# A decoder layer on one core: smaller blocks in the delta rule's substitution, and the memory keys worked out earlier

## The chip, the core and the metric

The kernel runs on one core of a Trainium2 chip. The time is the device time of one execution in microseconds. Three runs of the kernel before took 1222.79, 1224.20 and 1224.33 us; the median is 1224.2 us. The profile is of one execution, whose span is 1222.4 us.

## The reference

One layer of a hybrid decoder works on 512 tokens of 1024 channels, in float32. Each part is h = h + weight * rms_norm(part(rms_norm(h))). The parts are, in order: a SwiGLU feed-forward network with an inner width of 2816; a mixer; a cross-attention into 256 memory tokens (4 heads of 256); and a second feed-forward network.

The mixer has two groups of heads. Eight heads of 64 do causal softmax attention with a forget gate ("fox"). Four heads of 128 follow the gated delta rule, here over chunks of tokens:

```
L = strict_lower((k * beta) @ k.T) * decay       # per head and chunk
A = I + L
u = solve(A, v * beta);  w = solve(A, k * beta * exp(g))
for each chunk:
    v_new = u - w @ state
    o     = (q * exp(g)) @ state + attn_intra @ v_new
    state = state * exp(g_last) + k_tail.T @ v_new
```

The memory keys are the first half of rms_norm(mem) @ mem_w_kv. They depend on the memory tokens and weights alone, not on h.

## The kernel before, in words

The layer lies in SBUF as four blocks of 128 tokens: `h[0]` to `h[3]`, each 128 x 1024. Every product is float32 made of three passes over float32r parts: each weight block (128 x 1024, 512 KB) is loaded into `raw`, and split into a high part `wh` (ScalarE) and a low part `wl` (VectorE, or GpSimd for every second block where `nblock[1]` is 2; lines 431 to 436). `raw` has three buffers, `wh` and `wl` four each, and they go round in the order in which the program names the blocks, whatever the order of the work.

The order of the work is not the program's. The class `Issue` keeps every instruction with what it reads and writes, and at the end `settle` places them on the engines by assumed durations (lines 160 to 179 and `AFTER`) in ten rounds of list scheduling, and fixes the order in which each engine and the SP queue issue. On the chip an engine issues in that order: an instruction that is ready waits behind one that is not. Work on one PSUM bank stays in program order.

The mixer stage is, in program order:

- Gates: the first weight block gives the gate logits; a chain of small VectorE instructions on `gw` ends in `yd`, which TensorE transposes.
- For each of four delta heads: the keys' product, a convolution (`cy`, `cth`, `co`), and `L`, four chunks of 128 x 128 side by side.
- The inverse of A. `L` of each head is written to DRAM (`dl`), and its 32 x 32 diagonal blocks are read back into `Lb`, a block to a partition, 64 partitions for four heads, four chunks and four blocks (lines 983 to 987). Forward substitution on all 64 blocks at once takes 31 steps of two VectorE instructions, on `Wb` and `Tb` (lines 992 to 998). `inverse(hh)` writes a head's 16 inverted blocks to DRAM (`dt`, four DMAs), reads them back as `T` in place, transposes to `X`, and doubles the blocks twice by products, 32 to 64 and 64 to 128 rows (lines 1038 to 1092).
- `qv(hh)`: queries and values of a delta head, and its attention inside a chunk. `scan(hh)`: the recurrence over four chunks, a serial chain between TensorE, VectorE and ScalarE. `fox_values`: values of the fox heads.
- These steps stand in program order by `PLAN` (line 30): q0 q1 q2 i0 s0 i1 s1 q3 F0 i2 s2 i3 s3, where q is `qv`, i `inverse`, s `scan`, F `fox_values`.
- Then the fox heads in four pairs, the output gate `gz`, the normed and transposed memory tokens `mT` (lines 1292 to 1317), the output projection `wout`, and h's update.

The cross-attention then works out the memory keys `Km` (8 weight blocks `wkvk`, lines 1337 to 1355), the memory values `Vm` (8 blocks `wkvv`), and the queries, which need the norm of the new h. Keys and values need no h.

Of the kernel before, what the change touches and what calls it, by code (L numbers as in the profile page):

```python
# [16 lines left out]
P = 128  # L17
S = 512
# [20 lines left out]
class Issue:  # L39
    """The order in which the engines issue.  # L40

    Every instruction is kept with what it reads and writes. At the end they are placed on the
    engines by a rough cost, backwards and forwards by turns, of those ready the most urgent
    first, and each engine gets its instructions in that order (as dependencies that need no
    semaphore).
    """

    # from the end of an instruction to the start of one that waits for it: on the same engine,
    # on the tensor engine, on another
# [45 lines left out]
    def cells(self, x):  # L95
        """name, pieces touched, rows, free size"""
# [22 lines left out]
    def add(self, ins, unit, op, fp32):  # L119
# [4 lines left out]
        for group, cells_of, size_of in ((ins.ins, reads, sizes[0]), (ins.outs, writes, sizes[1])):  # L124
            for x in group:
# [5 lines left out]
                if name.startswith("psum"):  # L131
                    # one after another on a bank
# [127 lines left out]
class _Issuer:  # L260
    """an engine whose instructions are kept"""
# [19 lines left out]
def tile_decoder_layer(  # L281
# [23 lines left out]
    cid32: bass.AP,  # L305
# [14 lines left out]
    # slots of [128, 512], handed out by hand  # L320
# [20 lines left out]
    def move(src, dst, n=None):  # L341
        """free slots from one ring to another"""
# [14 lines left out]
    def bank(*ids):  # L357
        """the next PSUM bank of a ring of banks"""
# [20 lines left out]
    # that of some instructions stays as written  # L379
# [33 lines left out]
    def rstd_of(s0, s1):  # L413
        """(s0 + s1 + eps) ^ -1/2"""
# [16 lines left out]
    def wblock(ap):  # L431
        """now and then Pool takes the low part"""
# [10 lines left out]
    # the first loads, in the order in which they are needed  # L443
# [28 lines left out]
    def prenorm(src, g, dst):  # L472
        """rms_norm of a block of 128 rows, transposed and split into dst(half, part)."""
# [78 lines left out]
    def residual_epilogue(gidx, weight, nxt, final=False):  # L552
        """evac callback: h += weight * rms_norm(product) * gain; then nxt(t)."""
# [356 lines left out]
    for hh in range(GH):  # L910
        Q.dma_start(rows_of(dt_[hh]), zb)
# [660 lines left out]
```

## Time and profile before

| what | from the page or the times |
|---|---|
| median of three runs | 1224.2 us |
| span of the profiled execution | 1222.4 us |
| lies around it (1222.79 to 1224.33 less the span) | 0.4 to 1.9 us |
| TensorE matmul busy | 1192.9 us, 98% |
| VectorE busy | 642.7 us, 53% |
| ScalarE busy | 493.0 us, 40% |
| GpSimd busy | 128.6 us, 11% |
| moved by DMA | 120.32 MB, mean 98 GB/s |

Busy time of TensorE is the union of its matmuls, which overlap; a stretch at 20.00 of 20.00 us has no idle time, but is not free of slow matmuls. The stages by time: first feed-forward network to about 377 us, mixer to about 640 us with the delta rule at about 400 to 555 us, output projection to 689 us, cross-attention to about 860 us, second feed-forward network to the end.

### The profile page before, as it was taken

How to read it: one execution, taken by the hardware profiler on the slowest of the kernel's cores; microseconds unless marked ns; L12 is line 12 of the kernel's file. 1: busy time of each engine (PE TensorE's matmuls, PEld its weight loads, DVE VectorE, ACT ScalarE, POOL GpSimd, SP SyncE). 2: the span in 40 equal slices, each digit the busy share in tenths (PEclk: the TensorE clock that was granted, in tenths of full speed). 3: DMA queues.
4: the chain of work that ended last, by engine and by line, in shares of the span. 5: the costliest groups of instructions: out<-in, count | busy, mean ns of one | idle time of the engine just before them, and what ended most of it. 6: DMA issues, size and time to landing. Idle time of an engine off the chain costs nothing.

```text
span 1222.4 us, 15630 instructions
## 1 busy us (share of the span) xinstructions
PE 1192.9 (98%) x6078; PEld 1002.6 (82%) x6078; DVE 642.7 (53%) x1152; ACT 493.0 (40%) x1024; POOL 128.6 (11%) x121
## 2 busy tenths in 40 slices
PE   7999999999999899899999999999999999999997
PEld 7888888888888687788787888888988888888886
DVE  5655455442327979469975744546634334342323
ACT  5323223222226564368974644435422323222221
POOL 1000000000001432222020442012000000000000
PEclk9999999999999999999999999999999999999999
DMA  5332322333333231211214253222432332333321
GB/s 192 122 100 90 103 88 102 103 103 104 109 101 104 87 113 57 91 54 54 73 60 164 91 181 118 79 67 65 125 103 88 102 97 93 104 107 100 102 71 69
DMA packets 41753, 120.32 MB, mean 98 GB/s; under 512 B 9424, under 2 KB 9680, under 8 KB 41680
## 3 DMA queue, kind: packets, MB, share of 16 engines
q1 hardware_dynamic: 41168, 119.20, 30.9%
q8 instruction: 47, 0.77, 0.3%
q0 software_dynamic: 512, 0.13, 0.1%
q14 instruction: 26, 0.21, 0.1%
HBM read 114.73 MB, written 4.46 MB: 98 GB/s over the span
## 4 chain that ended last, share of the span: by engine, by line
PE 87%; DVE 7%; DMA 2%; issue 2%; ACT 2%; SPq 0%; POOL 0%; DVEq 0%; POOLq 0%; ACTq 0%
PE psum L270 87%; DVE Wb L270 1%; DVE Tb L270 1%; DMA mr<-in_mem_dram 1%; DVE wl L270 1%; DVE gw L270 1%; DMA raw<-in_wkvk_dram 1%; DVE co L270 1%; DVE xn L270 1%; DVE cy L270 0%; SPq L270 0%; DMA h<-in_x_dram 0%; DVE smalls L270 0%; DVE pt L270 0%; DVE h L270 0%
## 5 line engine op out<-in xcount | busy, mean ns | idle before, releaser
L270 PE MATMUL psum<-xt,wh 128*128 128x512 f32 (+1 forms) x2064 | 599.4, 374 | 0.3 <-ACT wh L270 0.2
L270 PEld LDWEIGHTS psum<-xt,wh 128*128 128x128 f32 x2064 | 373.6, 190 | 63.5 <-ACT wh L270 0.5
L270 ACT ACTIVATE wh<-raw 128x1024 fp32r<-128x1024 f32 (+1 forms) x202 | 213.0, 1056 | 526.0 <-PE psum L270 293.3
L270 PE MATMUL psum<-xt,wl 128*128 128x512 f32 (+1 forms) x1016 | 376.6, 375 | 0.8 <-DVE wl L270 0.7
L270 DVE TENSOR_TENSOR wl<-raw,wh 128x1024 fp32r<-128x1024 f32 (+1 forms) x176 | 216.3, 1230 | 275.8 <-ACT wh L270 275.2
L270 PEld LDWEIGHTS psum<-xt,wl 128*128 128x128 f32 x1016 | 190.9, 190 | 32.7 <-DVE wl L270 1.2
L270 PE MATMUL psum<-wh,hh 128*128 128x512 f32 x352 | 137.1, 390 | 0.0
L270 PE MATMUL psum<-wl,hh 128*128 128x512 f32 x352 | 137.1, 390 | 0.0
L270 PE MATMUL psum<-wh,hl 128*128 128x512 f32 x352 | 137.0, 389 | 0.0
L270 POOL TENSOR_TENSOR smalls<-smalls,mhalf 128x1 f32<-128x1 f32 (+1 forms) x38 | 26.5, 700 | 789.8 <-ACT smalls L270 784.0
L270 PEld LDWEIGHTS psum<-wh,hh 128*128 128x128 f32 x352 | 66.1, 188 | 13.8
L270 PEld LDWEIGHTS psum<-wh,hl 128*128 128x128 f32 x352 | 66.1, 188 | 13.6
L270 PEld LDWEIGHTS psum<-wl,hh 128*128 128x128 f32 x352 | 66.1, 188 | 13.6
L270 POOL TENSOR_TENSOR wl<-raw,wh 128x1024 fp32r<-128x1024 f32 x26 | 63.7, 2450 | 120.8 <-ACT wh L270 110.2
L270 PE MATMUL psum<-wh,xt 128*128 128x512 f32 x128 | 43.5, 409 | 0.4 <-DVE q L270 0.4
L270 DVE SCALAR_TENSOR_TENSOR hv<-s,psum 128x512 f32<-128x512 f32 x22 | 15.1, 688 | 53.7 <-PE psum L270 53.5
L270 DVE TENSOR_TENSOR tu<-psum,rb 128x512 f32<-128x512 f32 x22 | 15.2, 692 | 53.4 <-PE psum L270 53.3
L270 DVE TENSOR_TENSOR fg<-psum,gbc 128x512 f32<-128x512 f32 x32 | 22.0, 688 | 37.1 <-ACT u L270 37.1
L270 DVE TENSOR_TENSOR tg<-psum,rb 128x512 f32<-128x512 f32 x22 | 15.2, 692 | 44.5 <-PE psum L270 44.5
L270 ACT ACTIVATE u<-psum 128x512 f32<-128x512 f32 x32 | 19.0, 593 | 41.4 <-PE psum L270 41.4
L270 ACT ACTIVATE hh<-hv 128x512 fp32r<-128x512 f32 x44 | 27.4, 623 | 16.2 <-DVE hv L270 16.2
L270 DVE TENSOR_TENSOR hl<-hv,hh 128x512 fp32r<-128x512 f32 x44 | 30.1, 685 | 1.5 <-ACT hh L270 1.5
(232 smaller groups left out, 1431.3 us busy)
## 6 DMA issues: line engine op xcount, KB each, us to landing
raw<-in_f2gu_dram SPq DMA_DIRECT2D x44, 512.0 KB
raw<-in_f1gu_dram SPq DMA_DIRECT2D x43, 512.0 KB
raw<-in_f1d_dram SPq DMA_DIRECT2D x22, 512.0 KB
raw<-in_f2d_dram SPq DMA_DIRECT2D x22, 512.0 KB
raw<-in_wmt_dram SPq DMA_DIRECT2D x21, 512.0 KB
gbc<-in_gains_dram SPq DMA_DIRECT2D x16, 256.0 KB
raw<-in_wmn_dram SPq DMA_DIRECT2D x8, 512.0 KB
raw<-in_wout_dram SPq DMA_DIRECT2D x8, 512.0 KB
```

Source lines behind the costliest of these rows:

```text
L270: r = call(*args, **kw)
```

## The change

The substitution works on 16 x 16 diagonal blocks: 128 blocks, one to each partition, 15 steps instead of 31. The DRAM copies hold the chunks one after another, so that one DMA reads or writes all blocks of a head. `inverse` gets one more doubling ahead of the two, 16 to 32 rows, on 32 x 32 quarters with a mask.

The memory tokens are normed and transposed right after the `L`s, in the buffers of `h`; the memory keys become steps K0 to K3 of `PLAN`, ahead of i2. R0 gives free slots back. For that time h is kept in DRAM: each block is written after the first feed-forward network, and read back ahead of `wout`. The fox values lie in the buffers of h too. NSLOT grows by 3.

The durations that the planner assumes change: 13.3 ns instead of 2.6 ns over the columns for one-pass matmuls, half for four-pass matmuls of up to 32 rows, and 2.04 ns per element for the scan instruction. Comments are taken out.

```diff
-NSLOT = 51
+NSLOT = 54
-PLAN = 'q0 q1 q2 i0 s0 i1 s1 q3 F0 i2 s2 i3 s3'.split()
+PLAN = 'q0 q1 q2 i0 s0 i1 s1 q3 R0 F0 K0 K1 K2 K3 i2 s2 i3 s3'.split()
+KHOME = {}
...
-            cost = max(size * passes * 0.41667, cols * 0.8333) + 2.6
+            cost = max(size * passes * 0.41667, cols * 0.8333) + (13.3 if passes == 1 else 2.6)
+            if passes == 4 and rows <= 32:
+                cost /= 2
...
-            cost = 68 + size * (6.3 if op == "reciprocal" else 0.521 if single else 1.042) + 61 * scalars
+            each = {"reciprocal": 6.3, "tensor_tensor_scan": 2.04}.get(op, 0.521 if single else 1.042)
+            cost = 68 + size * each + 61 * scalars
...
+        def nxt(t):
+            norm(t)
+            kept.append(issue.tile(dram, [P, D], F32, tag="hd", bufs=4, name=nm("hd"), grain=(0, 1024)))
+            Q.dma_start(kept[t], h[t])
...
-        Q.dma_start(rows_of(dl[hh]), L)
-        for c in range(NT):
-            p0 = 16 * hh + 4 * c
-            Q.dma_start(Lb[p0 : p0 + 4], blocks_of(dl[hh], c))
+        Q.dma_start(rows_of(dl[hh]), by_chunk(L))
+        Q.dma_start(Lb[32 * hh : 32 * hh + 32], blocks_of(dl[hh]))
...
+    gkv = issue.tile(pool, [P, D], F32, tag="h0", name=nm("gkv"))
+    xns = issue.tile(pool, [P, D], F32, tag="h3", name=nm("xns"))
+    Q.dma_start(gkv, gains[G_MEMKV : G_MEMKV + 1, :].to_broadcast([P, D]))
+    for t in range(2):
+        mr = issue.tile(pool, [P, D], F32, tag=f"h{1 + t}", name=nm("mr"))
+        Q.dma_start(mr, mem[t * P : (t + 1) * P, :])
...
-    for j in range(31):
-        n = [64, 31 - j, j + 1]
-        w_ = Wb[0:64, 0 : n[1] * n[2]].rearrange("p (r s) -> p r s", s=n[2])
+    for j in range(15):
+        n = [P, 15 - j, j + 1]
+        w_ = Wb[:, 0 : n[1] * n[2]].rearrange("p (r s) -> p r s", s=n[2])
...
-        for c in range(NT):
-            p0 = 16 * hh + 4 * c
-            Q.dma_start(blocks_of(dt_[hh], c), Tb[p0 : p0 + 4])
+        Q.dma_start(blocks_of(dt_[hh]), Tb[32 * hh : 32 * hh + 32])
...
+        quarters = [slice(32 * i, 32 * i + 32) for i in range(4)]
+        qp = pg()
+        for c in range(NT):
+            for b in quarters:
+                mm(qp[b, 32 * c : 32 * c + 32], ck(L, c)[b, b], ck(X, c)[b, b], start=True, stop=True)
+        V.tensor_tensor(c3(Qs[:, 0:P]), c3(qp[:, 0:P]), low16[:, None, :].to_broadcast([P, NT, 32]), ALU.mult)
+        xp = pg()
+        for c in range(NT):
+            for b in quarters:
+                mm(xp[b, 32 * c : 32 * c + 32], ck(T, c)[b, b], Qs[b, 32 * c : 32 * c + 32], start=True, stop=True)
+            for b in quarters[0:3]:
+                mm(xp[b, P + 32 * c : P + 32 * c + 32], Qs[b, 32 * c : 32 * c + 32], ck(T, c)[b, b], start=True, stop=True)
+        for i, b in enumerate(quarters):
+            V.tensor_tensor(c3(X)[b, :, b], c3(X)[b, :, b], c3(xp[:, 0:P])[b], ALU.subtract)
+            if i < 3:
+                V.tensor_tensor(c3(T)[b, :, b], c3(T)[b, :, b], c3(xp[:, P : 2 * P])[b], ALU.subtract)
...
+    def memory_keys(dp):
+        ps = acc()
+        for e in range(2):
+            wh, wl = wblock(wkvk[2 * dp + e])
...
+            Km[0][dp], Km[1][dp] = u(F32R, "km"), u(F32R, "km")
+        split(Km[0][dp], Km[1][dp], ps)
...
+    for t in range(NT):
+        h[t] = issue.tile(pool, [P, D], F32, tag=f"h{t}", name=nm("h"))
+        Q.dma_start(h[t], kept[t])
```

## Rows read from the trace of the kernel before

**Rows 1.** The page: busy time, share and instructions of each engine; GB/s in 40 slices.

```profile
PE 1192.9 (98%) x6078; PEld 1002.6 (82%) x6078; DVE 642.7 (53%) x1152; ACT 493.0 (40%) x1024; POOL 128.6 (11%) x121
...
GB/s 192 122 100 90 103 88 102 103 103 104 109 101 104 87 113 57 91 54 54 73 60 164 91 181 118 79 67 65 125 103 88 102 97 93 104 107 100 102 71 69
```

**Rows 2.** Windows: stretch, length, busy per engine (instructions), granted clock, DMA share, GB/s.

```profile
400.00:420.00 20.00, 15.95 (x83) 13.22 (x82) 19.18 (x46) 11.16 (x32) 5.54 (x5) 0.91 0.29 92
460.00:480.00 20.00, 17.37 (x81) 13.82 (x80) 19.01 (x36) 10.47 (x28) 4.59 (x3) 0.91 0.18 53
500.00:520.00 20.00, 17.64 (x177) 14.12 (x178) 8.32 (x23) 9.09 (x33) 2.34 (x1) 0.91 0.35 113
640.00:660.00 20.00, 19.16 (x96) 15.15 (x95) 13.38 (x22) 9.76 (x21) 2.12 (x4) 1.00 0.67 220
```

**Rows 3.** Timeline of TensorE at its stalls: start, us, instructions, idle time before, what ended it.

```profile
410.80 1.08 PE L270 MATMUL psum<-ident,yd 128*128 128x128 f32 x4 [4.05 <-DVE smalls L270]
463.13 0.49 PE L270 MATMUL psum<-cm 128*128 128x512 f32 x1 [2.63 <-ACT vb L270]
502.32 0.52 PE L270 MATMUL psum<-X,L 32*32 32x32 f32 x8 [3.28 <-DVE X L270]
...
708.97 0.66 PE L270 MATMUL psum<-ident,xn 128*128 128x128 f32 x4 [1.86 <-DVE xn L270]
```

**Rows 4.** Windows of VectorE at the substitution: all of it, then `Tb`'s instructions alone.

```profile
448.00:495.00 47.00, 45.16 (x88) 0.96 0.19 61
...
448.00:495.00 47.00, 29.96 (x62) 0.96 0.19 61
```

**Rows 5.** Timeline of VectorE: steps of the substitution, and what stands between them.

```profile
449.72 0.21 DVE L270 TENSOR_TENSOR Tb<-Tb,Wb 64x60 f32<-64x60 f32 x1
457.39 2.46 DVE L270 TENSOR_TENSOR Wb<-Lb,Tb 64x207 f32<-64x207 f32 x1
459.88 0.37 DVE L270 TENSOR_TENSOR Tb<-Tb,Wb 64x207 f32<-64x207 f32 x1
```

**Rows 6.** Timeline of GpSimd beside it.

```profile
457.11 2.50 POOL L270 TENSOR_TENSOR wl<-raw,wh 128x1024 fp32r<-128x1024 f32 x1
```

**Rows 7.** Timeline of SP after the substitution, and the chain's piece behind it.

```profile
494.96 3.80 SPq L270 DMA_DIRECT2D dt<-Tb  x9
...
498.87 2.65 DMA T<-dt
```

**Rows 8.** TensorE by form, 380 to 620 us; then its timeline around small products.

```profile
L270 PE MATMUL psum<-X,L 32*32 32x32 f32 x64 | 3.4, 196 | 3.3 <-DVE X L270 3.3
...
506.30 0.47 PE L270 MATMUL psum<-X,L 32*32 32x32 f32 x13
506.70 0.51 PE L270 MATMUL psum<-wl,xt 128*128 128x512 f32 x1
507.04 0.63 PE L270 MATMUL psum<-wh,xt 128*128 128x512 f32 x2
```

**Rows 9.** Tiles `mT`, `mr`, `T`: operation, count, ns min/median/max, first and last start.

```profile
L270 PE MATMUL psum<-mT,wh x128: 277/283/365, 689.0 to 716.3; 128*128 128x256 f32 x128
L270 PE MATMUL psum<-wh,mT x64: 389/389/396, 716.5 to 738.1; 128*128 128x512 f32 x64
L270 DVE TENSOR_TENSOR mT<-psum,mT x8: 418/422/425, 649.5 to 654.4; 128x256 fp32r<-128x256 f32 x8
L270 DVE SCALAR_TENSOR_TENSOR xn<-mr,smalls,gbc x4: 743/748/752, 643.4 to 648.8; 128x512 f32<-128x512 f32 x4
L270 DVE TENSOR_SCALAR T<-psum x4: 283/283/284, 506.8 to 538.3; 32x128 f32<-32x128 f32 x4
```

**Rows 10.** Timeline of VectorE where the mixer begins: h's update, weight split, idle time.

```profile
381.12 0.74 DVE L270 SCALAR_TENSOR_TENSOR h<-fg,smalls,h 128x512 f32<-128x512 f32 x1
385.50 1.22 DVE L270 TENSOR_TENSOR wl<-raw,wh 128x1024 fp32r<-128x1024 f32 x1
393.88 0.75 DVE L270 SCALAR_TENSOR_TENSOR cy<-psum,cw,cy 128x511 f32<-128x511 f32 x1 [5.64 <-ACT cth L270]
```

More of the change, by code (lines that the diff above doesn't have):

```diff
@@ L304, in tile_decoder_layer @@
     crow: bass.AP,
-    cid32: bass.AP,
+    cid16: bass.AP,
     out: bass.AP,
@@ L715, in next_norm, with norm_and_store @@
         return nxt
-    ffn(f1gu, f1d, xT, G_F1POST, next_norm(G_MIXPRE), lead=lead_in)
+    kept = []
+    def norm_and_store(gidx):
+        norm = next_norm(gidx)
+        def nxt(t):
+            norm(t)
+            kept.append(issue.tile(dram, [P, D], F32, tag="hd", bufs=4, name=nm("hd"), grain=(0, 1024)))
+            Q.dma_start(kept[t], h[t])
+        return nxt
+    ffn(f1gu, f1d, xT, G_F1POST, norm_and_store(G_MIXPRE), lead=lead_in)
     xT = state["xT"]
@@ L983, in tile_decoder_layer @@
         fr(Dn)
-        Q.dma_start(rows_of(dl[hh]), L)
-        for c in range(NT):
-            p0 = 16 * hh + 4 * c
-            Q.dma_start(Lb[p0 : p0 + 4], blocks_of(dl[hh], c))
+        Q.dma_start(rows_of(dl[hh]), by_chunk(L))
+        Q.dma_start(Lb[32 * hh : 32 * hh + 32], blocks_of(dl[hh]))
         front.append((kT, L, cV, cR, kt))
-    for j in range(31):
-        n = [64, 31 - j, j + 1]
-        w_ = Wb[0:64, 0 : n[1] * n[2]].rearrange("p (r s) -> p r s", s=n[2])
+    mTt = [[[u(F32R, "mT") for _ in range(2)] for _ in range(2)] for _ in range(2)]
+    gkv = issue.tile(pool, [P, D], F32, tag="h0", name=nm("gkv"))
[4 more added lines that the diff above has]
+        Q.dma_start(mr, mem[t * P : (t + 1) * P, :])
+        sq = [small(1) for _ in range(2)]
+        hs = [slice(j * 512, (j + 1) * 512) for j in range(2)]
+        xn = [xns[:, hs[j]] for j in range(2)]
+        for j in range(2):
+            square(mr[:, hs[j]], 1.0 / 32.0, sq[j], xn[j])
+        r = rstd_of(*sq)
+        for j in range(2):
+            V.scalar_tensor_tensor(xn[j], mr[:, hs[j]], r, gkv[:, hs[j]], ALU.mult, ALU.mult)
+            tp = acc()
+            for c in range(4):
+                TE.transpose(ck(tp, c), ck(xn[j], c), ident)
+            t3 = tp.rearrange("p (c q) -> p c q", c=4)
+            for e in range(2):
+                hi, lo = (
+                    mTt[j][q_][e].rearrange("p (c q) -> p c q", c=2)[:, :, t * P : (t + 1) * P] for q_ in range(2)
+                )
+                split(hi, lo, t3[:, 2 * e : 2 * e + 2, :])
+    for j in range(15):
+        n = [P, 15 - j, j + 1]
+        w_ = Wb[:, 0 : n[1] * n[2]].rearrange("p (r s) -> p r s", s=n[2])
         V.tensor_tensor(
@@ L1153, in evac_fv @@
         def evac_fv(n, t, ps):
-            Vf[t] = [u(F32R, "v") for _ in range(2)]
+            v_ = issue.tile(pool, [P, D], F32R, tag=f"h{t}", name=nm("v"))
+            Vf[t] = [v_[:, j * 512 : (j + 1) * 512] for j in range(2)]
             for j in range(2):
@@ L1159, in fox_values, with mk, spare @@
         nat_product(range(KD), lhs_x, wmn[1:2], 1, evac_fv, 0)
+    def mk(k, q_, sl=slice(0, 256)):
+        base = (k % 2) * 256
+        return mTt[k // 4][q_][(k % 4) // 2][:, base + sl.start : base + sl.stop]
+    Km = [[None] * 4 for _ in range(2)]
+    def memory_keys(dp):
+        ps = acc()
+        for e in range(2):
+            wh, wl = wblock(wkvk[2 * dp + e])
+            n = 0
+            for k in range(KD):
+                ws = slice(k * P, (k + 1) * P)
+                for w, q_ in ((wh, 0), (wh, 1), (wl, 0)):
+                    mm(
+                        ps[:, e * 256 : (e + 1) * 256],
+                        w[:, ws],
+                        mk(k, q_),
+                        start=(e == 0 and n == 0),
+                        stop=(n == 3 * KD - 1),
+                        skip_group_check=True,
+                    )
+                    n += 1
+        if dp in KHOME:
+            km = issue.tile(pool, [P, D], F32R, tag=KHOME[dp], name=nm("km"))
+            Km[0][dp], Km[1][dp] = km[:, 0:512], km[:, 512:1024]
+        else:
+            Km[0][dp], Km[1][dp] = u(F32R, "km"), u(F32R, "km")
+        split(Km[0][dp], Km[1][dp], ps)
+    def spare(n):
+        for r_ in ("cy", "co", "kt", "gf"):
+            move(r_, "m")
+    steps = {
+        'q': qv,
+        'i': inverse,
+        's': scan,
+        'F': lambda _: fox_values(),
+        'K': memory_keys,
+        'R': spare,
+    }
     for step in PLAN:
-        {'q': qv, 'i': inverse, 's': scan, 'F': lambda _: fox_values()}[step[0]](int(step[1]))
+        steps[step[0]](int(step[1]))
     fr(Gk, Gq)
@@ L1261, in tile_decoder_layer @@
     fr(Fk, Fq, cm, zmask)
-    for p_ in Vf:
-        fr(*p_)
     nblock[1] = 0
@@ L1430, in tile_decoder_layer @@
             aTm.append(at)
-        fr(*qT_[0], *qT_[1], *ptm[0], *ptm[1], Km[0][hd], Km[1][hd])
+        fr(*qT_[0], *qT_[1], *ptm[0], *ptm[1])
+        if hd not in KHOME:
+            fr(Km[0][hd], Km[1][hd])
     for p_ in Vm.values():
@@ L1535 @@
     )
-    cmask, crow, cid32 = _consts(np)
+    cmask, crow, cid16 = _consts(np)
     arrs = dict(
@@ L1558 @@
         crow=crow,
-        cid32=cid32,
+        cid16=cid16,
     )
```

96 lines of the change are left out of this document (28 added, 68 removed).

## The prediction, made before the changed kernel ran

> **What bounds the kernel now.** I read the page first, for the engine that is never idle: TensorE is busy for 1192.9 of 1222.4 us, VectorE, the next, for 642.7 [rows 1]. So time can be won in two ways only: fewer products, or less idle or half-clocked time of TensorE. The change removes no large product, so I looked for the second, in windows of 20 us over the mixer. The reader is to see three windows in which TensorE is short of 20.00 and its granted clock is 0.91 instead of 1.00 [rows 2]. A mean of 0.91 between the levels of 1.2 and 2.4 GHz costs 0.09 x 20 = 1.8 us in each. The timeline of TensorE then names the stalls: 4.05 us at 410.80, for the gates' chain; 2.63 us at 463.13, for `vb`, so that a PSUM bank comes free; 3.28 us at 502.32, for `X`, the first inverse [rows 3]. In each case the engine was full until then, sat idle, and the lower clock followed.
>
> The stall at 502.32 stands behind the substitution. Between 448 and 495 us VectorE is busy for 45.16 of 47 us, and 29.96 of these are the 62 instructions of the substitution [rows 4]. Then SP issues nine block DMAs for 3.80 us, and the read of `T` takes another 2.65 us [rows 7]. The stall at 463.13 has the same origin: the convolution's last step `co` is queued on VectorE behind substitution steps, one of which takes 2.46 us where its twin takes 0.37 [rows 5]. Beside the long one GpSimd makes a low part for 2.50 us [rows 6].
>
> **The substitution.** 62 instructions become 30, on 128 partitions instead of 64. A step j has (15-j)(j+1) elements to a partition, at most 64; a step of 60 elements takes 0.21 us [rows 5]. 30 x 0.21 = 6.3 us against 29.96, so VectorE gains 23.7 us. It was full there, so the inverse comes earlier by about as much. SP's block DMAs ahead of the first `T` shrink from nine to one or two, some 3 us less at 3.80/9 = 0.42 us each [rows 7]. The read and the write of a head still have to land, about 2.65 us each. `X` is then ready some 25 us before TensorE has used up its other work, and the stall at 502.32 goes: 3.28 + 1.8 = 5.1 us. With VectorE no longer full, `co` isn't late, and the stall at 463.13 goes: 2.63 + 1.8 = 4.4 us. Together 9.5 us; the bounds are 0 and 9.5.
>
> **The added doubling.** Per head 16 + 16 + 12 = 44 products of 32 x 32, 176 in all. Thirteen of the kind take 0.47 us, the last of them 0.19, so one starts every 0.28/12 = 23 ns [rows 8]: 176 x 23 = 4.1 us of TensorE. Each head's two new groups also break into the stream of large products. The first large product after small ones is followed after 0.34 us (506.70 to 507.04, [rows 8]) where 0.227 us is usual: the values' 96 products take 21.6 us [rows 9]. So 0.11 us at the exit, as much taken for the entry, 8 x 0.22 = 1.8 us. In all +5.9 us. If products of different quarters overlap more the 4.1 is 2; by the mean of 3.4/64 = 53 ns of busy time [rows 8] it is 9.4.
>
> The Trainium skill ("TensorEngine Tiling (Array Packing)", Key Properties) has it that a change of tiling mode drains the engine while tiles of one mode run independently. The trace shows both, 0.11 us at a change and 23 ns between small products; by its theoretical sixteenfold the products themselves would be nearly free and the sum 4 us better.
>
> VectorE gets 8 more instructions per head, 32 at about 0.28 us, the price of `T<-psum` on 32 rows [rows 9]: 9 us, spread over four inverses, and some 3 us more latency for each. It lies beside TensorE's other work: VectorE has 8.32 of 20 us to do between 500 and 520 [rows 2]. Without that cover a head's 3 us would be a stall once for each pair of heads, 6 us.
>
> **The memory keys.** 192 products of 256 columns, three for each two of the row with 128, run from 689.0 to 716.3 [rows 9]: 27 us, with 1.86 us of waiting and the norm's transposes between, so some 24 us of their own. They move, so TensorE's sum doesn't change; what changes is what they hide. In the delta rule they add 24 us of work that waits for no scan, behind the fox values, by the order of the weight buffers. Taken away they leave the values alone (21.6 us) to hide h's update and norm. That chain ended at 708.97, 20 us after the keys began, and with 1.86 us of idle time even so [rows 3]; the values cover the same 20 us, so I change nothing there. If the cover is short by the 1.86 again, that is as before. The memory tokens' own norm leaves the stretch at 640, where TensorE is idle for 0.84 us [rows 2]; I take -0.8.
>
> Its VectorE work, 4 x 0.75 + 8 x 0.42 = 6.4 us [rows 9], goes to about 388, where VectorE is idle for 5.64 us [rows 10], or into the 23.7 us set free. In the gates' chain it would lengthen the stall at 410.80 by up to 6.4 us.
>
> **h in DRAM.** Eight transfers of 512 KB, each 2.7 us at the 192 GB/s of the first slice. The stores follow the updates, the last at 381.12 [rows 10]; the slices there move 101 to 104 GB/s [rows 1], which leaves room. A weight block behind one store is 2.7 us later, and the last of the first four is split at 385.50 [rows 10]. The loads need the fox values' buffers and fall before the output projection. I cost both at nothing; without cover 2.7 us for each store ahead of a weight block.
>
> **The assumed durations.** A matmul of 512 columns was assumed at 215.9 ns, and now at 226.6, where the trace has 227. It changes the order, and I price it at nothing, bounds in the rivals.
>
> **The sum.** -9.5 + 5.9 - 0.8 = -4.4 us on the span of 1222.4 us: 1218.0. The median lies 1.8 us over this span, so 1219.8 us.
>
> **The rivals.** *More stalls go.* With TensorE's durations right, the planner may also cure the order at 410.80 and at 708.97 [rows 3]. The first is worth 4.05 + 1.8, the second 1.86: 1219.8 - 7.7 = 1212.1. For it: the head's own products were left over when TensorE stopped at 406. Against it: the gates' chain itself is not touched, and the keys can't be used there, since their weights come after all of q.
>
> *One stall comes back.* The fixed order makes TensorE wait for something in the delta rule, 4.8 us: 1224.6, no change. For it: each inverse has two more hand-overs and the planner takes a DMA's 2.1 us for what took 2.65. Against it: 45 us of fox values and keys can be put between.
>
> *Both come back: slower.* This is one mechanism: TensorE's order is fixed by assumed durations, and VectorE's real ones are longer when GpSimd works beside it, 2.46 for 0.37 us [rows 5, 6]. So far TensorE ran slower than planned, by 11 ns for each large product, some 2.8 us over the 260 products from 440 to 500 us, and so came late to its waits. With true durations this cover is gone, and every late `X` or `vb` is a stall at full length, with the lower clock behind it. The place is the delta rule, from 440 to 530 us, the price the 9.5 us: 1229.3. It decides from 6.8 us on, that is when nearly both stalls are back. Against it: VectorE has 23.7 us less to do there.
>
> The Trainium skill ("SBUF — State Buffer", Who interferes with whom) says that a VectorE instruction with two SBUF inputs and a GpSimd instruction that reads SBUF exclude each other for the whole instruction. The pair at 457 us agrees [rows 5, 6]. By this rule the four GpSimd splits of the keys' weights bring four more collisions of about 2.1 us into the stretch, 8.4 us of VectorE; it speaks for this rival.
>
> That the keys stay where they were is not possible: the weight buffers go round in program order.
>
> **How the numbers follow.** Forecast 0.42, more stalls gone 0.17, one back 0.20, both back 0.16, outside all 0.05. A measurement of this kernel can tell 0.2%, 2.4 us, from no change. The forecast's own range is 1216 to 1223 (the doubling at 2 or at 9), so 0.36 of its 0.42 is faster; with the second case and a share of the rest, faster 0.55. Same has the remainder of the forecast and most of one back, 0.23. Slower is 0.22. The range runs from just under the second case to the last one: 1211 to 1229.
>
> **What would show it.** VectorE's sum for `Tb` should be near 6 us and end before 470 us; no idle time over 1 us of TensorE before `X` or a `vb`; windows with clock 0.91 at 400 alone; small products' starts 20 to 25 ns apart; the keys' matmuls between 490 and 540 us; TensorE full through the values. I am wrong if a new wait of more than 2 us stands in the delta rule, if the stall at 410.80 grows by VectorE work on the memory tokens, or if the values end before the norm does.

## The result, and the profile after

The changed kernel takes 1238.1 us (median of four runs, 1235.9 to 1241.1). Beside it the kernel before took 1224.3 us. The ratio is 1.012 with a 95% interval of 1.0098 to 1.0142: slower by 13.9 us, where 4.4 us of gain were forecast. The profiled execution has a span of 1238.3 us, 15.9 us more than before. It is one of two at 1240.4 and 1241.1 us with a mean granted clock of 0.989, beside two at 1235.9 with 0.993 and 0.994; the profile before is of an execution at 0.995, where the median of the kernel's 95 runs beside the experiments is 0.992, so the two profiles differ more by the clock than the medians do.

First the page, the engines' sums, to be held against [rows 1]:

```profile
PE 1208.5 (98%) x6430; PEld 1009.7 (82%) x6430; DVE 631.9 (51%) x1152; ACT 495.0 (40%) x1024; POOL 129.8 (10%) x121
```

TensorE has 352 more instructions and 15.6 us more busy time. VectorE has 10.8 us less to do. The bound is the same engine.

Where are the 15.9 us? A product that both kernels have in common tells it, the last one of the memory values. These are TensorE's timelines (start, duration, operation), after and then before:

```profile
754.03 0.39 PE L274 MATMUL psum<-wh,mT 128*128 128x512 f32 x1
754.25 0.61 PE L274 MATMUL psum<-xt,wh 128*128 128x512 f32 x2
```

```profile
738.09 0.39 PE L270 MATMUL psum<-wh,mT 128*128 128x512 f32 x1
738.32 0.61 PE L270 MATMUL psum<-xt,wh 128*128 128x512 f32 x2
```

It starts 15.94 us later. So nothing is lost behind it, and the loss lies between the end of the first feed-forward network (376.8 us before, 376.2 after) and here.

The windows of 20 us, columns as in [rows 2]:

```profile
400.00:420.00 20.00, 16.41 (x83) 12.57 (x82) 18.69 (x43) 12.56 (x30) 7.09 (x5) 1.00 0.37 115
420.00:440.00 20.00, 17.89 (x90) 14.36 (x90) 15.30 (x40) 13.38 (x52) 7.30 (x6) 0.83 0.19 54
460.00:480.00 20.00, 18.27 (x208) 14.07 (x208) 15.71 (x38) 9.84 (x25) 4.58 (x3) 1.00 0.33 86
500.00:520.00 20.00, 20.00 (x118) 17.08 (x117) 13.51 (x35) 9.95 (x36) 5.16 (x4) 1.00 0.19 57
...
560.00:580.00 20.00, 20.00 (x123) 16.24 (x122) 6.16 (x19) 8.35 (x27) 3.65 (x4) 0.75 0.09 28
640.00:660.00 20.00, 18.87 (x101) 15.12 (x100) 17.45 (x62) 15.89 (x48) 1.55 (x3) 1.00 0.17 51
720.00:740.00 20.00, 14.84 (x70) 11.71 (x68) 16.69 (x18) 12.00 (x24) 13.26 (x7) 1.00 0.51 158
740.00:760.00 20.00, 19.87 (x85) 16.57 (x86) 8.29 (x11) 8.35 (x11) 4.81 (x2) 0.91 0.50 151
```

Three things are to be seen. The window at 500, which had the stall for `X`, is full and at clock 1.00: that forecast held. The window at 560 is full too, and yet its clock is 0.75: TensorE has no idle time there and half of it runs at 1.2 GHz. The window at 720 has 5.16 us of idle time, in the memory values, where the kernel before had none.

TensorE's timeline names the waits of the changed kernel (the bracket is the idle time before the instruction and what ended it):

```profile
409.68 0.63 PE L274 MATMUL psum<-ident,yd 128*128 128x128 f32 x4 [1.90 <-DVE yd L274]
424.38 0.40 PE L274 MATMUL psum<-Mgl,ones 128*128 128x16 f32 x2 [2.11 <-DVE Mgl L274]
470.13 0.66 PE L274 MATMUL psum<-ident,co 128*128 128x128 f32 x4 [1.73 <-DVE co L274]
474.17 0.45 PE L274 MATMUL psum<-X,L 32*32 32x32 f32 x32
593.64 0.69 PE L274 MATMUL psum<-k,q 128*128 128x256 f32 x2 [1.99 <-DVE smalls L274]
740.13 0.75 PE L274 MATMUL psum<-ident,xn 128*128 128x128 f32 x4 [4.42 <-DVE xn L274]
```

The first small product, `X,L` at 474.17, has no wait: before it had 3.28 us, at 502.32 [rows 3]. New are the waits for `Mgl`, `co` and `k,q`, and the wait for `xn`, the norm of the new h, has grown from 1.86 [rows 3] to 4.42 us.

The substitution did what was forecast. This is VectorE in the window from 448 to 470, for `Tb` alone:

```profile
448.00:470.00 22.00, 9.80 (x30) 1.00 0.31 82
```

It takes 9.80 us instead of 29.96 [rows 4]; 6.3 were forecast. One step of it took 2.35 us, again beside a low part that GpSimd made for 2.40 us, and the 29 others 0.26 us on average.

An account of TensorE goes by the interval from each instruction's start to the next start. The 32 x 32 products have 9.4 us of these intervals instead of 4.7, so the 352 added instructions take 4.65 us. All other instructions are held against the median interval of their form in the kernel before; the excess over the medians, which is idle and half-clocked time, grew by 11.2 us. Up to the first `X` it fell by 3.6; to the first fox head it grew by 6.2; in the fox heads by 5.0; from the end of the output projection to the last value by 4.7; elsewhere it fell by 1.1. Of these 3.4, 1.7 and 1.7 us, in the second, third and fourth stage, are longer time at 1.2 GHz.

### The profile page after: what moved, and what is told of

It is laid out like the page before. It is cut to its first block, busy times and chain, and to the rows that moved or that the text cites. A ratio compares the mean times of both kernels' runs of the same rounds, so it can differ in the third digit from the quotient of the medians.

```text
span 1238.3 us, 16319 instructions
## 1 busy us (share of the span) xinstructions
PE 1208.5 (98%) x6430; PEld 1009.7 (82%) x6430; DVE 631.9 (51%) x1152; ACT 495.0 (40%) x1024; POOL 129.8 (10%) x121
## 4 chain that ended last, share of the span: by engine, by line
PE 86%; DVE 7%; ACT 2%; DMA 2%; issue 2%; POOL 1%; SPq 0%; DVEq 0%; POOLq 0%; ACTq 0%
PE psum L274 86%; DVE wl L274 1%; DVE xn L274 1%; DVE gw L274 1%; ACT wh L274 1%; DVE h L274 1%; DVE cy L274 1%; DVE Wb L274 1%; DVE xt L274 0%; DVE p L274 0%; DMA hd<-h 0%; POOL smalls L274 0%; DMA raw<-in_wout_dram 0%; ACT k L274 0%; DMA raw<-in_wkvv_dram 0%
## 5 line engine op out<-in xcount | busy, mean ns | idle before, releaser
L274 POOL TENSOR_TENSOR smalls<-smalls,mhalf 128x1 f32<-128x1 f32 (+1 forms) x38 | 29.2, 770 | 472.5 <-ACT smalls L274 463.8
L274 PEld LDWEIGHTS psum<-wh,hl 128*128 128x128 f32 x352 | 66.1, 188 | 13.7
L274 PEld LDWEIGHTS psum<-wh,hh 128*128 128x128 f32 x352 | 66.1, 188 | 13.7
```

Of the source, the lines that this page charges most:

```text
L274: r = call(*args, **kw)
```

## The experiments

The first four kernels each undo or do one part.

**The assumed durations** were put back in the changed kernel (d1), and put alone into the kernel before (d2):

```diff
-            cost = max(size * passes * 0.41667, cols * 0.8333) + (13.3 if passes == 1 else 2.6)
-            if passes == 4 and rows <= 32:
-                cost /= 2
+            cost = max(size * passes * 0.41667, cols * 0.8333) + 2.6
...
-            each = {"reciprocal": 6.3, "tensor_tensor_scan": 2.04}.get(op, 0.521 if single else 1.042)
-            cost = 68 + size * each + 61 * scalars
+            cost = 68 + size * (6.3 if op == "reciprocal" else 0.521 if single else 1.042) + 61 * scalars
```

> The changed kernel with the assumed durations of before (blocks of 16, keys in the delta rule, h in DRAM stay). Theory A, the keys' move costs: the time stays near the changed kernel's 1238, at 1233 to 1239, and TensorE again stalls in the norm ahead of the queries and runs at half clock around the last two inverses. Theory B, the new durations cost by taking cover from TensorE's waits: 1226 or less. Theory C, the added doubling costs: as under A, 1233 to 1239.

> The kernel before with the new assumed durations alone. Theory A (keys' move): 1222 to 1227. Theory B (durations): 1230 to 1236, with longer stalls before the first inverse and vb. Theory C (doubling): 1222 to 1227.

**The blocks of 16 rows alone** (d3, lines 895 to 1092 as in the change, with the mask and the constants) and **the memory keys alone** with the memory tokens and h in DRAM (d4) were put into the kernel before, with its own durations. This line is d4's:

```diff
-PLAN = 'q0 q1 q2 i0 s0 i1 s1 q3 F0 i2 s2 i3 s3'.split()
+PLAN = 'q0 q1 q2 i0 s0 i1 s1 q3 R0 F0 K0 K1 K2 K3 i2 s2 i3 s3'.split()
```

> The kernel before with blocks of 16 rows alone: keys, h and durations as before. Theory A (keys' move): 1219 to 1226, the stalls at vb and X gone, 5 us of products added. Theory B (durations): the same 1219 to 1226. Theory C (the added doubling and its switches cost some 10 us): 1231 to 1237.

> The kernel before with the memory keys and tokens in the delta rule and h in DRAM alone: substitution on 32 rows, durations of before, 51 slots. Theory A: 1231 to 1238, a stall of 4 to 6 us in the norm behind the output projection, where GpSimd makes low parts for the values. Theory B and C: 1221 to 1227.

| kernel | median us | ratio to before, 95% |
|---|---|---|
| d1, change with old durations | 1232.9 | 1.0061 (1.0041 to 1.0080) |
| d2, new durations alone | 1230.0 | 1.0059 (1.0034 to 1.0085) |
| d3, blocks of 16 alone | 1239.7 | 1.0104 (1.0066 to 1.0143) |
| d4, keys alone | 1235.2 | 1.0084 (1.0069 to 1.0099) |

No part is a gain. The durations, priced at nothing, cost 5 to 6 us both ways. The losses don't add: 5.5, 15 and 11 are not 13.9. The windows show why, here of d3 and of d4:

```profile
480.00:500.00 20.00, 18.07 (x143) 14.07 (x144) 6.62 (x21) 5.01 (x17) 0.59 (x1) 0.62 0.09 27
...
540.00:560.00 20.00, 20.00 (x120) 16.78 (x120) 3.98 (x12) 6.07 (x21) 0.00 (x0) 0.59 0.00 1
```

```profile
500.00:520.00 20.00, 17.72 (x135) 12.36 (x134) 4.42 (x10) 5.58 (x17) 2.34 (x1) 0.68 0.39 115
520.00:540.00 20.00, 18.88 (x131) 17.83 (x130) 10.39 (x26) 9.64 (x31) 3.15 (x2) 0.81 0.20 67
```

The granted clock is 0.6 to 0.7 over whole windows, in d3 at 540 with TensorE busy for 20.00 of 20.00 us. TensorE's timeline of d3 shows how such a stretch begins, at the inverse of a head: idle for 1.36 us, then small products, then single large ones between small ones.

```profile
484.66 0.55 PE L270 MATMUL psum<-Qs,T 32*32 32x32 f32 x9 [1.36 <-DVE T L270]
...
486.83 0.79 PE L270 MATMUL psum<-xt,wh 128*128 128x512 f32 x1
487.43 0.63 PE L270 MATMUL psum<-xt,wl 128*128 128x512 f32 x1
487.98 1.67 PE L270 MATMUL psum<-Qs,T 32*32 32x32 f32 x16
```

In the kernel before the stall for `X` was followed by one such stretch of 3.4 us. In d3 there are stretches of 17.1 and 20.5 us, in d4 one of 20.5, in the changed kernel one of 10.2 (559.7 to 569.9). Products of 512 columns start 427 ns apart there, and 227 ns elsewhere (medians in d3), so a microsecond at 1.2 GHz loses about half of one. I therefore separate a kernel's time into the loss at the lower clock and the rest. The loss is the span times (1 less the mean granted clock), as a mean over all runs; the rest is the median time less this loss. The clock is on record to three digits, so one run's loss is known to some 0.6 us:

| kernel | median us | lost by the clock | rest |
|---|---|---|---|
| before | 1224.6 | 9.3 | 1215.3 |
| after | 1238.1 | 10.8 | 1227.3 |
| d1, old durations | 1232.9 | 9.8 | 1223.0 |
| d2, durations alone | 1230.0 | 12.0 | 1218.0 |
| d3, blocks of 16 alone | 1239.7 | 19.8 | 1219.9 |
| d4, keys alone | 1235.2 | 19.7 | 1215.5 |

The keys alone lose nothing but the clock (10.4 us). The blocks of 16 alone lose 10.5 by the clock and 4.6 otherwise. In the changed kernel the clock is 1.5 us worse than before, and 12.0 us are lost at any clock. The loss differs between executions of one kernel in one order: the clock is from 0.984 to 0.995 in the eight of d2 (20 to 6 us), while all four of d3 (0.981 to 0.987) and of d4 (0.983 to 0.985) are low. The profile of d2 is of the execution at 0.984.

The next four runs test the suspects, and how far an order drawn anew moves the time. **No added doubling** (n1) leaves the doubling from 16 to 32 rows out, so that the inverse is incomplete:

```diff
-        qp = pg()
-        for c in range(NT):
-            for b in quarters:
-                mm(qp[b, 32 * c : 32 * c + 32], ck(L, c)[b, b], ck(X, c)[b, b], start=True, stop=True)
...
-                V.tensor_tensor(c3(T)[b, :, b], c3(T)[b, :, b], c3(xp[:, P : 2 * P])[b], ALU.subtract)
```

> The changed kernel without the added doubling: its 44 products and 8 VectorE updates per head are left out, so the inverses are incomplete; all else as changed. Clock theory (small products among few large ones let the granted clock fall to half and keep it there without idle time): the loss at half clock between the first inverse and the fox heads, 5.1 us in the changed kernel, goes to 2 or less, and with the products' 5 us the time falls by 8 to 11 us, to 1227 to 1230. Rival, the products cost only their own 23 ns each and their switches: 5 to 6 us less, 1232 to 1233. Rival, the order alone decides: the time may move either way by several us with the half-clock stretches elsewhere.

**The values' low parts on VectorE** (n2) takes GpSimd's splits away from the norm; the planner still counts them on GpSimd, so that the order stays the changed kernel's:

```diff
+    GV = _Issuer(nc.vector, "POOL", issue, False, "DVE")
...
-        return wsplit(wload(ap), G if nblock[1] and nblock[0] % nblock[1] == 0 else V)
+        return wsplit(wload(ap), (GV if asdve[0] else G) if nblock[1] and nblock[0] % nblock[1] == 0 else V)
```

> The changed kernel with the low parts of the memory values' weights all on VectorE; the planner still counts every second one on GpSimd, so each engine keeps the order of the changed kernel. Norm theory (the norm of h is late since its VectorE instructions wait for GpSimd's low parts): h and xn of 2.9 us fall to 0.75, the stall of 4.42 us ahead of the norm's last transposes falls to 2.5 or less, and the time by 2 to 5 us, to 1233 to 1236. Rival, the norm is late for ScalarE and the weights' loads: the stall stays at 4 us and the time at 1238.

**Another rounding** draws another order: 3.1 for 2.6 ns in the kernel before (n3), 12.8 for 13.3 ns in the changed one (n4).

> A control: the kernel before with 3.1 instead of 2.6 ns assumed over a matmul's columns, which says nothing new of the chip. If the parts' losses are their own, 1223 to 1226. If the order of before is one good draw of the planner among many (lottery theory): 1228 to 1236, with other stalls and more time at half clock.

> The same control on the changed kernel: 12.8 instead of 13.3 ns. If the changed kernel's loss is its own, 1236 to 1240. Lottery theory: anywhere from 1226 to 1242.

| kernel | median us | ratio to before, 95% | lost by the clock | rest |
|---|---|---|---|---|
| n1, no doubling | 1228.5 | 1.0023 (1.0005 to 1.0041) | 8.7 | 1219.8 |
| n2, low parts on VectorE | 1229.5 | 1.0039 (1.0018 to 1.0061) | 7.1 | 1222.3 |
| n3, before, other order | 1227.3 | 1.0027 (1.0004 to 1.0049) | 11.0 | 1216.3 |
| n4, after, other order | 1241.4 | 1.0128 (1.0088 to 1.0168) | 12.7 | 1228.7 |

The loss is not the luck of one order: n4 has it too, and a new order moved these two kernels by about 3 us. Leaving the doubling out gave 9.6 us where 5.9 were forecast, in an order that is drawn anew as well. The 5.1 us that the changed kernel's profile loses at half clock between the first `X` and the fox heads are gone in n1; but they are gone in n2 too, whose TensorE issues the same products in the same order. So n1 does not show that the small products bring the lower clock.

Taking GpSimd away from the norm gives 8.7, more than the 2 to 5 that were expected, of which 3.7 are the clock and 5.0 the rest. The edit itself is worth less. At the first `ident,gx`, ahead of the first instruction that it changes, TensorE in n2's profile is 9.0 us ahead already; from there to the last value (754.03 in the changed kernel) it gains 4.0 us. The changed kernel first, then n2:

```profile
674.98 0.71 PE L274 MATMUL psum<-ident,gx 128*128 128x128 f32 x5
...
665.99 0.71 PE L276 MATMUL psum<-ident,gx 128*128 128x128 f32 x5
...
741.03 0.39 PE L276 MATMUL psum<-wh,mT 128*128 128x512 f32 x1
```

What the edit takes away is seen in the changed kernel, VectorE first and then GpSimd:

```profile
728.53 1.41 DVE L274 SCALAR_TENSOR_TENSOR xn<-h,smalls,gbc 128x512 f32<-128x512 f32 x2 [0.44 <-POOL smalls L274]
729.86 3.56 DVE L274 SCALAR_TENSOR_TENSOR h<-fg,smalls,h 128x512 f32<-128x512 f32 x2
...
737.25 3.49 DVE L274 SCALAR_TENSOR_TENSOR xn<-h,smalls,gbc 128x512 f32<-128x512 f32 x2 [0.44 <-POOL smalls L274]
```

```profile
729.26 2.94 POOL L274 TENSOR_TENSOR wl<-raw,wh 128x1024 fp32r<-128x1024 f32 x1 [0.25 <-ACT wh L274]
735.82 1.40 POOL L274 TENSOR_TENSOR smalls<-smalls,mhalf 128x1 f32<-128x1 f32 x1 [3.61 <-ACT smalls L274]
737.19 2.33 POOL L274 TENSOR_TENSOR wl<-raw,wh 128x1024 fp32r<-128x1024 f32 x1
```

A pair of these instructions takes 1.41 us where it begins ahead of a low part, and 3.56 and 3.49 behind the start of one: 2.1 us each, in series ahead of the last `xn`. The low part at 729.26 is in the way of h's update, that at 737.19 in the way of the norm itself. In n2 the waits for `xn` are shorter, 1.76 and 0.91 us instead of 0.87 and 4.42:

```profile
727.61 0.66 PE L276 MATMUL psum<-ident,xn 128*128 128x128 f32 x4 [1.76 <-DVE xn L276]
729.41 0.66 PE L276 MATMUL psum<-ident,xn 128*128 128x128 f32 x4 [0.91 <-DVE xn L276]
```

The third batch asks whether the doubling's price is its small tiles. **On whole chunks** (w1), with a mask of 128 columns, three VectorE instructions instead of eight:

```diff
-            for b in quarters:
-                mm(qp[b, 32 * c : 32 * c + 32], ck(L, c)[b, b], ck(X, c)[b, b], start=True, stop=True)
+            mm(ck(qp, c), ck(L, c), ck(X, c), start=True, stop=True)
...
+            mm(ck(xp, c), ck(T, c), ck(Qs, c), start=True, stop=True)
...
+            mm(ck(tq, c), ck(Qs, c), ck(T, c), start=True, stop=True)
```

w2 adds n2's edit, w3 also d1's; w4 is d3 with the doubling on whole chunks.

> The changed kernel, but the added doubling is done with 12 products of 128 x 128 for each head (whole chunks, one mask of 128 columns) instead of 44 products of 32 x 32, and with 3 VectorE instructions instead of 8. TensorE's own time for it hardly changes: 12 x 0.11 = 1.3 us a head against some 1.0 us. My theory, that the small products cost far more than their own time (they run with gaps and at the lower granted clock, and their hand-overs are many): the time falls by 5 to 10 us against the changed kernel, to 1228 to 1233, and the half-clock stretch at 560 us is gone or shorter. The rival, that the price of the doubling is its place in the order and its two hand-overs to VectorE, which stay: 1235 to 1241.

> As the run with whole chunks, and the low parts of the values' weights are all made by VectorE. Theory (the two losses are separate: the doubling, and the norm of h that meets GpSimd's low parts): the gains add up, some 5 us below the run with whole chunks, 1223 to 1228, and the wait of TensorE for xn is under 2 us. Rival (the norm is late because the delta rule ends late, so what helps one helps the other): no faster than the run with whole chunks.

> As the run with both edits, and with the assumed durations of the kernel before. The changed kernel gained some 5 us from the old durations. Theory (the new durations are a loss of their own, by a tighter order): 1218 to 1224, faster than before or the same. Rival (which durations are used only draws another order, good or bad by a few us): anywhere within 5 us of the run with both edits, above as well as below.

> The kernel before with the blocks of 16 rows alone, the added doubling on whole chunks (12 products of 128 x 128 a head). With the products of 32 x 32 this took 1239.7. Theory (small products among few large ones hold the clock at its lower level): 1222 to 1231, and the stretches of 17 and 20 us at half clock, without idle time, are gone. Rival (the clock falls because the delta rule's dependent steps are closer together, whatever their size): 1235 to 1241, with stretches of half clock of 15 us and more.

| kernel | median us | ratio to before, 95% | lost by the clock | rest |
|---|---|---|---|---|
| w1, after, whole chunks | 1236.9 | 1.0098 (1.0067 to 1.0129) | 7.4 | 1229.5 |
| w2, and low parts on VectorE | 1235.8 | 1.0091 (1.0055 to 1.0127) | 8.3 | 1227.5 |
| w3, and old durations | 1231.1 | 1.0043 (1.0027 to 1.0058) | 5.1 | 1226.0 |
| w4, blocks of 16 alone, whole chunks | 1228.6 | 1.0027 (1.0014 to 1.0040) | 4.0 | 1224.6 |

w4 against d3 came out as the theory has it: 11 us less, the clock's loss down from 19.8 to 4.0, no stretch over 3.4 us. But its order is another one too, and o1 below gets as much from an order alone. The windows of w4 at the same places:

```profile
480.00:500.00 20.00, 20.00 (x200) 16.55 (x201) 9.96 (x25) 10.07 (x34) 1.08 (x1) 1.00 0.10 28
...
540.00:560.00 20.00, 20.00 (x112) 17.26 (x111) 11.44 (x32) 14.47 (x42) 4.05 (x4) 1.00 0.10 28
```

w1, w2 and w3 went to the rivals' side. One reason is that I had the price of a whole chunk wrong. TensorE's timeline of w1: a product of 128 x 128 is two instructions, eight take 1.05 us.

```profile
470.74 1.05 PE L274 MATMUL psum<-X,L 128*128 128x128 f32 x8
```

The 96 added instructions start 112 ns apart: 10.7 us, not 5. So w1 trades 6 us of excess for some 7 us of products. In w2 the wait for `xn` fell from 4.45 to 1.84 us as in n2, and the stretch from the first `ident,gx` to the last value from 80.2 to 76.7. The time fell by 1.1 us alone; with four runs of each between 1233 and 1241 us that does not tell the edit's worth.

The last six runs. **A compact doubling** has no small tiles and fewer columns: the four 32 x 32 blocks of a chunk stand one under another in 32 columns, and `X` is made from `T` again by VectorE:

```diff
+            mm(qp[:, 32 * c : 32 * c + 32], ck(T, c), Qs[:, 32 * c : 32 * c + 32], start=True, stop=True)
+        V.transpose(Qs[:, P : 2 * P], qp[:, 0:P])
...
+            mm(xp[:, 32 * c : 32 * c + 32], ck(X, c), Qs[:, P + 32 * c : P + 32 * c + 32], start=True, stop=True)
...
+            V.tensor_tensor(c3(T)[b, :, b], c3(T)[b, :, b], c3(xp[:, 0:P])[b], ALU.subtract)
+        V.transpose(X, T)
```

k1 is d3 with it, k2 the changed kernel with it, k4 the changed kernel with it and the edits of n2 and d1. k3 is n1 and n2 together (so without the added doubling).

> The kernel before with the blocks of 16 rows alone, where the added doubling is done on compact blocks: 8 products of 128 rows and 32 columns for each head, with no 32 x 32 tiles, and X made from T again by VectorE. With 32 x 32 products this took 1239.7, with whole chunks 1228.6, of which 10.7 us are the whole chunks' products. Theory (the price of the doubling is its small tiles, the stalls forecast to go do go): 1228.6 - 10.7 + 2 to 3 = 1219 to 1222, faster than before, with no stretch of half clock over 7 us. Rival (any closely dependent small work there lets the clock fall, whole chunks were only big enough to hold it): 1230 to 1240 with stretches of 15 us and more.

> The changed kernel with the compact doubling (8 products of 128 rows and 32 columns for each head). Theory (the small tiles are the loss at the doubling, the norm's loss of some 5 us stays): 1226 to 1231, as without the doubling (1228.6). Rival (the place between the postponed inverses and the keys is the loss): 1235 to 1240.

> The changed kernel without the added doubling (the inverse stays incomplete) and with the values' low parts all made by VectorE. Each alone gave 9 us. Theory (two separate losses that are nearly the whole of the 13.9 us): 1219 to 1224. Rival (both runs won by the same thing, a luckier order or clock): 1226 to 1231, as each alone.

> The changed kernel with the compact doubling, the values' low parts on VectorE, and the assumed durations of before. The same with whole chunks took 1231.1, with 10.7 us of products of 128 x 128. Theory: 1231.1 - 10.7 + 2 to 3 = 1222 to 1225, no slower than before. Rival (the small products bring the half clock back): 1230 to 1238.

o1 and o2 are d3 and d4 with 3.1 for 2.6 ns, as n3:

> The kernel before with the blocks of 16 rows alone, with 3.1 for 2.6 ns in the assumed durations, so that another order is drawn. Theory (the 352 added small instructions bring the half clock, in whatever order): 1234 to 1242 again, stretches of half clock of 10 us and more within the inverses. Rival (the order brings it): 1222 to 1230, no stretch over 7 us.

> The kernel before with the memory keys moved and h in DRAM alone, with 3.1 for 2.6 ns, so that another order is drawn. My view here is the other way: no small product is added, so the stretch of 20.5 us belongs to the order: 1222 to 1230, no stretch over 7 us. Rival (the keys push the inverses together, whatever the order): 1233 to 1238 with a stretch of 15 us or more.

| kernel | median us | ratio to before, 95% | lost by the clock | rest |
|---|---|---|---|---|
| k1, blocks of 16 alone, compact | 1227.2 | 1.0018 (1.0002 to 1.0034) | 5.5 | 1221.7 |
| k2, after, compact | 1242.8 | 1.0148 (1.0123 to 1.0172) | 11.8 | 1231.0 |
| k3, no doubling, low parts on VectorE | 1226.0 | 1.0013 (1.0001 to 1.0026) | 7.3 | 1218.6 |
| k4, after, three edits | 1224.6 | 0.9999 (0.9986 to 1.0012) | 6.4 | 1218.2 |
| o1, d3 in another order | 1227.7 | 1.0033 (1.0020 to 1.0047) | 9.4 | 1218.3 |
| o2, d4 in another order | 1232.1 | 1.0057 (1.0039 to 1.0075) | 13.2 | 1218.8 |

- k1 missed its range by 5 us, again by the price of a product. Eight instructions of 32 columns take 0.97 to 1.08 us, as long as eight of 128 columns; 64 of them are 7.0 us by their starts, not 2 to 3. The excess over the medians is 6.8 us below the kernel before, in the two profiles: the stalls' gain, spent on these products. Its clock's loss is 5.5 us, and it has no long stretch:

```profile
476.08 1.08 PE L270 MATMUL psum<-Qs,T 128*128 128x32 f32 x8 [0.63 <-DMA T<-dt]
477.31 0.97 PE L270 MATMUL psum<-Qs,T 128*128 128x32 f32 x8
```

- k2 went to the rival's side and above it. Its order has a stall of 5.06 us for `yd`, and the 4.43 us for `xn`, as in the changed kernel. So with the new durations the loss stays when the doubling has no small tiles.
- k3 came out on the edge of the rival's range: 12.1 us of the 13.9 come back, less than the 18.3 of n1 and n2 added. The two gains overlap, though together they are nearly the whole: without GpSimd at the norm, leaving the doubling out gives 3.5 us (k3 against n2) instead of 9.6.
- k4 is level with the kernel before. It still carries 6.5 us of compact products; its excess over the medians is 6.6 us below the kernel before. That is a gain near the forecast one, spent on the doubling, as in k1. How much of it n2's edit brings is open, since the kernel before was not run with that edit. Its window in the values is full again:

```profile
720.00:740.00 20.00, 20.00 (x98) 16.64 (x97) 14.30 (x20) 13.76 (x21) 5.77 (x4) 1.00 0.67 199
```

- o1 is 12 us faster than d3, the rival's time, but it keeps a stretch of 13.7 us at half clock from 478.9, with no idle time in this window:

```profile
480.00:500.00 20.00, 20.00 (x146) 15.90 (x142) 7.60 (x19) 8.65 (x27) 1.09 (x1) 0.69 0.10 27
```

- o2 went against me: the stretch of 20.5 us stands in the other order as well, behind a stall of 2.63 us for `X`:

```profile
503.53 0.43 PE L271 MATMUL psum<-X,L 32*32 32x32 f32 x8 [2.63 <-DVE X L271]
```

So a long stretch needs no added product: n3, the kernel before in another order, has one of 13.7 us at 503.2, behind a wait of 1.81 us, and d2 one of 23.9. The stretches of 10 us and more (the changed kernel, d1 to d4, n3, w1, o1, o2) hold small products of an inverse, and in d2, d3, d4, n3, o1 and o2 begin behind an idle TensorE ahead of one; n4 has one of 10.2 us at 423.2 among other small products. What makes one of them 3.4 us and another 20 is not settled: the kernel before had the stall and only 3.4, and n2 had the changed kernel's order and no long stretch. No version here beats the kernel before.

All profiles together show where the wait for `xn` comes from. In d1, which has the old durations, VectorE is held up at the same two pairs for as long, but TensorE comes to the last transposes without a wait:

```profile
729.74 3.56 DVE L271 SCALAR_TENSOR_TENSOR h<-fg,smalls,h 128x512 f32<-128x512 f32 x2
736.14 3.57 DVE L271 SCALAR_TENSOR_TENSOR xn<-h,smalls,gbc 128x512 f32<-128x512 f32 x2 [0.45 <-POOL smalls L271]
```

```profile
674.68 0.71 PE L271 MATMUL psum<-ident,gx 128*128 128x128 f32 x5
...
739.25 0.60 PE L271 MATMUL psum<-ident,xn 128*128 128x128 f32 x4
...
746.74 0.39 PE L271 MATMUL psum<-wh,mT 128*128 128x512 f32 x1
```

It has started 66 of the values' 96 products by then, the changed kernel 45. So it is in all kernels with the keys moved; the last column is the stretch from the first `ident,gx` to the last value:

| durations, low parts of the values | kernels | products before the last transposes | stretch, us |
|---|---|---|---|
| new, GpSimd and VectorE | after, n1, n4, k2, w1 | 45 | 78.7 to 80.2 |
| new, VectorE alone | n2, k3, w2 | 45 | 75.0 to 76.7 |
| old, GpSimd and VectorE | d1, d4, o2 | 66 | 71.3 to 72.4 |
| old, VectorE alone | k4, w3 | 66 | 71.3 and 71.8 |

With the old durations GpSimd costs the stretch nothing that can be seen; with the new ones it costs 3.5 to 4 us, and the order some 4 more.

## Why the prediction was wrong

**The bound** was right: TensorE, and nothing behind the values moved.

**The stalls, -9.5: over-sized.** The mechanism held: VectorE's 29.96 us became 9.80, `X` came 28 us earlier, and the stalls at 502.32 and 463.13 went, with the lower clock behind them. But ahead of the first `X` only 3.6 us of excess were won, since other waits on VectorE came up, 2.11 for `Mgl` with 6.8 us at half clock behind it, and 1.73 for `co`. k1, w4 and o1, with the blocks of 16 alone, have 6.8, 7.3 and 5.9 us less excess in all than the kernel before, so in other orders some two thirds of the term were to be had.

**The added doubling, +5.9: mis-sized, by how much is open.** The 352 added instructions take 4.65 us, near the 4.1 of 176 x 23 ns, but by luck: a product is two instructions, and the row of thirteen [rows 8] counts instructions, so that 23 ns each would have made 8.1 us. They came 13 ns apart. The change of size and the waits were put at 1.8 us; n1 puts the whole at 9.6, k3 against n2 at 3.5. So the idle and half-clocked time around the small products lies between nothing and some 5 us, and no run fixes it. The Trainium skill ("TensorE: Matmul & The Clock Gate", Part 1) has the lower clock as the state after idleness. The trace shows it after idle time, at 740.6 for instance, but also for 10.2 us from 559.7 in which TensorE was never idle.

**The assumed durations, nothing: the step that failed.** The prediction said "I price it at nothing, bounds in the rivals". d1 gives 5.2 us back, d2 loses 5.5, and w3 is 4.7 us below w2. Most of it has its place at the norm: the order that the new durations draw puts the last transposes of `xn` behind 45 of the values' 96 products instead of 66, and TensorE waits 4.4 us for one `xn`, in the changed kernel, n1, n4, k2 and w1 alike. The stretch takes 79.05 us there and 72.06 in d1, half of the 13.9 us. In the two profiles these 7.0 are nearly all of the 7.5 us between d1 and the changed kernel; by the medians d1 gives back 5.2. Why the planner's order changed so is not shown.

**The norm behind the keys: the other half of this step.** "The values cover the same 20 us, so I change nothing there" held with the old durations, where the waits for `xn` are under 0.9 us (d1, d4, o2), and failed with the new ones. It took the cover by its length. But the cover is made of weights, and GpSimd's low parts of these weights hold up the norm that is to be covered, by 2 x 2.1 us. The kernel before has such a pair too, ahead of its wait of 1.86 us at 708.97 [rows 3]:

```profile
705.41 3.50 DVE L270 SCALAR_TENSOR_TENSOR xn<-h,smalls,gbc 128x512 f32<-128x512 f32 x2
```

It was said of the keys in the delta rule, by the rule of the Trainium skill ("SBUF — State Buffer", Who interferes with whom), and not of the values at the norm. The rows at 729 and 737 agree with that rule.

**The memory tokens' norm, -0.8,** did not come: in the 20 us from 675 us, where the output projection begins in the changed kernel, TensorE is idle for 0.85 us, as for 0.84 in the stretch at 640 before [rows 2].

```profile
675.00:695.00 20.00, 19.15 (x94) 15.70 (x93) 9.34 (x11) 7.66 (x11) 1.72 (x4) 1.00 0.71 233
```

**The slower rival** (0.16) had the right kind of mechanism, VectorE late where GpSimd works beside it under an order fixed by assumed durations, but at the wrong place: 440 to 530 us, where the stalls did not come back, instead of 720 to 740.

**The memory keys** are neutral but for the clock in d4, as forecast: the rest is 1215.5 against 1215.3. In o2, another order, it is 3.5 us above. That more time would be lost at the lower clock, 10.4 us in d4 and 3.9 in o2, was not foreseen. **h in DRAM** cost nothing that can be seen there. The wait for `yd`, feared to grow, fell from 4.05 [rows 3] to 1.90 us. The keys' products ran from 525.7 to 550.3, where 490 to 540 were forecast.

**What stays open.** The fox heads lost 5.0 us of the profile's 15.9, with 1.99 us for `k,q` and 3.4 us at half clock behind it. Every other order lost something there too, and no run ties it to a part. Of the loss between the first `X` and the fox heads no run says how much is the doubling, how much the order and how much the one execution's clock.

## What to carry to other kernels

Where one engine is the bound and is 98% busy, a stall that is won elsewhere is small change against what a new order can lose: price the order itself, by drawing it anew, before an edit of 4 us is believed: 0.5 ns in an assumed duration moved d3 by 12 us. Before a gain is put down to an edit, see in the trace whether it arises behind the first instruction that the edit changes. Small products are to be priced with what stands between them, since TensorE can run at its lower clock without ever being idle; look at the granted clock of full windows too. Before a piece of work is called cover, look at how much of it the order puts ahead of the wait, at what makes its inputs, and whether that holds up the thing to be covered.

## What the runs showed of the hardware

A float32 product that is not split into three passes is two instructions on TensorE, and over 128 rows they start 112 ns apart, with 32 columns (k1) as with 128 (w1). Instructions of 32 x 32 products on different quarters start 7 ns apart at the median (`Qs,T` in the changed kernel). The clock of 1.2 GHz stayed for up to 23.9 us (d2, from 501.0), and was 0.59 on average in a window in which TensorE was busy for 20.00 of 20.00 us (d3 at 540). Two VectorE instructions that read `h` and `gbc`, or `fg` and `h`, took 3.5 to 3.6 us beside a low part on GpSimd and 1.41 ahead of one.
